# First attention: three quarters of the probabilities transposed by DMA in 16-bit halves

## The chip, the cores and the metric

The kernel runs on one core of a Trainium2 chip. The core has five engines, each with an instruction queue of its own that is worked in order: TensorE (matmuls and weight loads, PE and PEld in the profile), VectorE (DVE), ScalarE (ACT), GpSimd (POOL) and SyncE (SP, which issues most DMAs). An instruction waits on semaphores for what it needs; while it waits, everything behind it on the same engine waits too. The metric is the device time of one execution in microseconds.

## The reference

A trunk of two layers on 256 tokens of width 1024, all in float32: a layer of dilated attention, a layer of forgetting attention, each followed by a SwiGLU feed-forward part, and a last norm. The change touches the first attention alone:

```python
DILATED_PATTERNS = ((128, 1), (512, 4), (2048, 16))

def dilated_mixer(h, w_in, w_out):
    B, S, _ = h.shape
    proj = (h @ w_in).reshape(B, S, N_GROUPS, 3, N_HEADS, HEAD_DIM)
    ...
    for g, (window, dil) in enumerate(DILATED_PATTERNS):
        q = partial_rotary(proj[:, :, g, 0], pos)
        k = partial_rotary(proj[:, :, g, 1], pos)
        v = proj[:, :, g, 2]
        o, lse = dilated_band_attention(q, k, v, dil, window // dil)
        ...
    wts = jax.nn.softmax(jnp.stack(lses, axis=0), axis=0)
    o = jnp.einsum('gbsh,gbshd->bshd', wts, jnp.stack(outs, axis=0))
    return o.reshape(B, S, ATTN_WIDTH).astype(h.dtype) @ w_out
```

The softmax over the three groups' denominators makes the whole the same as one softmax over the scores of all three groups together, which is how the kernel computes it.

## The kernel before

**Units.** The 16 heads are worked in four quads of four heads, a quad in two pairs (`pr`) of two heads (`h`). The loop over `a_units` takes one piece of weights (1024 x 256 values) at a time: for each quad six q and k pieces (three groups, `rotated` behind each) and the value pieces. A piece comes by two DMAs of 512 KB into `raw` tiles (five of them), issued on SyncE. ScalarE makes its high part `wh` (L79) and VectorE its low part `wl` (L83), and TensorE multiplies three times (`mm3`: high by high, high by low, low by high). Four pieces fit into the `wh` and `wl` tiles, so a piece is split well ahead of its use.

**A projection** of q or k is 48 matmuls of 256 columns into one of two accumulators `ps_mm`. VectorE empties it with a shuffle (L441) and a multiply (L442), and only then can the projection after next start.

**Attention of a quad.** `scores_0` and `scores_12` put the scores of a head into one tile `p` of five blocks of 128 columns: block 0 and block 4 for the dilated groups, blocks 1 to 3 for the first group. `softmax_a` (ScalarE's L288 and L505, VectorE's L496 and L507) makes probabilities of them in place. `trans_a` transposes a pair's ten blocks on TensorE (L300) into PSUM and copies them out (L305: two copies of 512 columns on ScalarE, one of 256 on VectorE). `pv_a` multiplies them with the values (L312). Blocks of values for the dilated groups are put together by GpSimd, 16 copies a quad (L284, `values_12`).

**Order.** `later(i, ...)` puts a step behind unit `i`. Softmax stands behind the first unit after a quad's last q or k projection; the transposes of the two pairs stand behind two units some four units later, and PV behind the unit after these. A scheduler places each engine's instructions from that program order; work under `first()` goes ahead of other work that is ready. The instructions of an engine then run in that fixed order.

Of the kernel before, what the change touches and what calls it, by code (L numbers as in the profile page):

```python
# [9 lines left out]

F32 = mybir.dt.float32
F32R = mybir.dt.float32r
AF = mybir.ActivationFunctionType
ALU = mybir.AluOpType
AX = mybir.AxisListType

P = 128
D = 1024
S = 256
# [12 lines left out]
def trunk(ctx: ExitStack, tc: tile.TileContext, T, out):  # L32
    nc = tc.nc
# [3 lines left out]
    ap = ctx.enter_context(tc.tile_pool(name="ap", bufs=1))  # L37
# [258 lines left out]
    def transposed(blocks, copy=nc.vector.tensor_copy, tag="tr", home="pt"):  # L296

        tr = psum(tag)
        for i, b in enumerate(blocks):
            nc.tensor.transpose(tr[:, i * P:(i + 1) * P], b, ident)  # L300
        n = len(blocks) * P
        bufs, cols = {"pt": (3, 512), "bias": (4, 6 * P)}[home]
        w = ap.tile([P, cols], F32, tag=home, name="pt", bufs=bufs)
        with first():
            copied["last"] = copy(w[:, :n], tr[:, :n])  # L305
        return w

    def pv(o, v, kb, pr, w, n, start, stop):

        for h in range(2):  # L310
            c = kb * S + pr * P + h * HD
            nc.tensor.matmul(o[h * HD:(h + 1) * HD], v[:, c:c + HD], w(h), start=start, stop=stop)  # L312
# [6 lines left out]
    o = psum("o")  # L319
# [55 lines left out]
    for k in range(KT):  # L375
        if k % 4 == 0:
            w = tuple(wp.tile([P, 2048], F32R, tag=y, name=y, bufs=4) for y in ("wh", "wl"))
        g, u = g_a[:, k:k + 1], slice(k % 4 * 512, k % 4 * 512 + 512)
        with first(), in_order(cut):
            if k == 0:  # L380
                a = nc.vector.tensor_scalar(hi[:, k], xk[k], g, None, op0=ALU.mult)
            else:
                a = nc.scalar.activation(hi[:, k], xk[k], AF.Copy, scale=g)
# [4 lines left out]
        if k in (1, 5, 7):  # L388
            with first(), in_order(cut):
                a = [square(i) for i in {1: (0, 1), 5: (2,), 7: (3,)}[k]][-1]  # L390
# [12 lines left out]
    with first(), in_order(cut):  # L403
        a = square(4)
# [22 lines left out]
    x = []  # L427
# [81 lines left out]
    def trans_a(quad, pr):  # L509
# [5 lines left out]
                         transposed([block(h, 3) for h in range(2)], home=home),  # L515
                         transposed([block(h, b * 4) for h in range(2) for b in range(2)], nc.scalar.copy, "o", home)]

    def pv_a(quad, pr):
        vs, ws = quad["v"], quad["w", pr]
        o = psum("o")  # L520

        pv(o[:, :S], vs[0], 0, pr, lambda h: ws[0][:, h * S:(h + 1) * S], S, True, False)
        pv(o[:, P:S], vs[0], 1, pr, lambda h: ws[1][:, h * P:(h + 1) * P], P, False, False)
        halves = lambda x, a: x.rearrange("p (b n) -> p b n", b=2)[:, :, a * 32:a * 32 + 32]
        for a in range(4):
            pv(halves(o[:, :S], a), vs[1 + a % 2], a // 2, pr, lambda h: halves(ws[2][:, h * S:(h + 1) * S], a), 64,
               False, a == 3)
        src = o[:, :S].rearrange("p (b a u) -> p b a u", b=2, a=4)
        kt = quad["hq"] * 2 + pr
        split(ot, lambda x: x[:, kt, :].rearrange("p (b u a) -> p b a u", a=4, b=2), src)  # L530
# [3 lines left out]
    def later(i, fn, *a):  # L534
        due.setdefault(i, []).append((fn, a))

    quads = [{"hq": hq, "fm": {}, "pt": {}, "v": {}} for hq in range(4)]
    for i, (hq, g, w) in enumerate(a_units):
        quad = quads[hq]
        if i == 3:  # L540
            o = o_next
        elif i:

            wt = weights("a_in", hq * 9 + g * 3 + w, read if i > 4 else None)
        if i != 3 and (w < 2 or g == 0 and hq > 1):
            o = psum("mm")
        if i == 1:
            ident = const("ident", [P, P])
            rcos = const("rcos", [P, S])
            rsin = const("rsin", [P, S])  # L550
        if i == 2:
            mask0 = const("mask0", [P, 3 * P])
            mask12 = const("mask12", [P, S])
        if i in (24, 31):
            x.append(hrow("x"))
            t = len(x) - 1
            nc.sync.dma_start(x[t], T["x"][t * P:(t + 1) * P, :])
        if w < 2:
            for c in range(2):
                if i == 3 and c == 0:  # L560
                    continue
                proj_feat(xt, wt, o[:, c * S:(c + 1) * S], c, (KT // 2, rstd_a) if i == 2 and c == 1 else None)
            if i == 2:
                values_12(quad["v"], lead)

                second = []
                wt = weights("a_in", 1, second)
                second.pop(0)()
                o_next = psum("mm")
                rb = psum("tr")  # L570

                def rows():
                    for t in range(2):
                        nc.tensor.matmul(rb[:, t * P:(t + 1) * P], r_a[t].to_broadcast([P, P]), ident,
                                         start=True, stop=True)

                proj_feat(xt, wt, o_next[:, :S], 0, (6, rows))
                with first():
                    for c in (rcos, rsin):
                        nc.vector.tensor_tensor(c, c, rb[:, :S], op=ALU.mult)  # L580
            q, read = rotated(o, g, w)
            if i == 2:
                second.pop()(read)
            quad["fm"][g, w] = q
            if w == 1:

                j = i + (hq == 0)
                step = lambda hq: 9 * hq + 11 + 2 * (hq == 0)
                if g == 0:
                    later(step(hq - 1) + 2 if hq else j + 3, scores_0, quad)  # L590
                if g == 2:
                    later(j + 1, scores_12, quad)
                    later(j + 1, softmax_a, quad)
                    for pr in range(2):
                        later(step(hq) + pr, trans_a, quad, pr)
                    for pr in range(2):
                        later(step(hq) + 2, pv_a, quad, pr)
        elif g == 0 and hq > 1:
            for t in range(2):
                proj_tok(xt, wt, o[:, t * S:(t + 1) * S], t)  # L600
            quad["v"][0] = v_tile(o, r_a)
        elif i > 1:


            half = hq % 2 if g == 0 else g - 1
            if half == 0:

                lead = [psum("mm" if g else "o") for _ in range(2)]
            proj_pair(xt, wt, lead, half)
            if half and g == 0:  # L610
                vs = [v_tile() for _ in range(2)]
                for t in range(2):
                    v_pair(vs, lead[t], t, r_a[t])
                for y in range(2):
                    quads[hq - 1 + y]["v"][0] = vs[y]
            elif half:
                values_12(quad["v"], lead)
        for fn, a in due.pop(i, ()):
            fn(*a)
# [289 lines left out]
    ws = [weights("b_in", i * 3 + 2, ahead=2 - i) for i in range(2)]  # L909
    os = [psum("mm") for _ in range(2)]  # L910
    vs = [v_tile() for _ in range(3)]
# [27 lines left out]
    for i, (hq, w) in enumerate(b_units):  # L939
# [4 lines left out]
        o = psum("mm")  # L944
        if w < 2:
# [15 lines left out]
            if w == 1:  # L961
                j = i + 1
# [38 lines left out]
    parts, hg = [], []  # L1001
# [111 lines left out]
```

## Time and profile before

| | us |
|---|---|
| median of 3 runs | 742.76 (742.75 to 742.82) |
| the profiled execution | 742.78 |
| its span in the trace | 741.0 |
| VectorE busy | 489.5 |
| ScalarE busy | 375.5 |
| GpSimd busy | 65.0 |

The profile is of one execution. Its page lists each engine's busy time, the chain of work that ended last, groups of instructions (source line, engine, operation, output and inputs, count, busy time, mean) and the DMAs. The timeline gives single instructions: start, duration, engine, line, operation, count, and in brackets how long the engine had been idle and who ended that. In the list of waits a row says which instruction waited for which other, the total, how often, and the longest. TensorE's granted clock is at nine tenths of full speed or more in 39 of the span's 40 slices, and at eight in the last.

The DMA queues and what else the prediction needs are shown there.

### The profile page before, as it was taken

Reading aid. Unit: us, or ns where it says so; the run is one execution under the profiler, and the core shown is the slowest. Engines: PE = TensorE matmul, PEld = TensorE weight load, DVE = VectorE, ACT = ScalarE, POOL = GpSimd, SP = SyncE. Lnnn points to the kernel's source line nnn. Section 1 sums busy time; section 2 is a strip of 40 time slices with the busy share of each in tenths; the row PEclk is TensorE's granted clock in tenths of the full one; section 3 lists DMA queues with packets and bytes.
Section 4 is the critical chain, followed back from the end, with each engine's and each line's share of the span. In section 5 each row is a group of like instructions: output and inputs, shape, how many; then the busy total and the mean of one; then the engine's idle time right before and its main releaser. Section 6 shows DMA issues by size and latency. Waiting matters only on the chain.

```text
span 741.0 us, 14364 instructions
## 1 busy us (share of the span) xinstructions
PE 733.1 (99%) x5916; PEld 679.1 (92%) x5916; DVE 489.5 (66%) x768; ACT 375.5 (51%) x617; POOL 65.0 (9%) x106
## 2 busy tenths in 40 slices
PE   9999999999999999999999999999999999999996
PEld 7999989999988789999999988999889999999995
DVE  6997988787888575545556375586877455555533
ACT  7546437437436465445445354487565444445521
POOL 0600003005006010000000004110000000000001
PEclk9999999999999999999999999999999999999998
DMA  8865544644646267565567543785537655656601
GB/s 332 304 199 172 188 156 147 212 154 150 214 145 225 65 226 251 180 201 194 184 209 234 170 133 123 261 254 170 171 118 236 227 187 193 206 177 217 206 1 57
DMA packets 39297, 138.00 MB, mean 186 GB/s; under 512 B 4512, under 2 KB 5696, under 8 KB 39232
## 3 DMA queue, kind: packets, MB, share of 16 engines
q1 hardware_dynamic: 39088, 136.94, 56.0%
q8 instruction: 46, 0.75, 0.4%
q14 instruction: 19, 0.16, 0.1%
q10 hardware_dynamic: 144, 0.15, 0.1%
HBM read 136.00 MB, written 1.07 MB: 185 GB/s over the span
## 4 chain that ended last, share of the span: by engine, by line
PE 96%; ACT 1%; DMA 1%; DVE 1%; issue 0%; SPq 0%; POOL 0%; POOLq 0%; DVEq 0%; ACTq 0%
PE ps_mm L207 34%; PE ps_mm L202 17%; PE ps_tr L207 9%; PE ps_sc L207 8%; PE ps_o L207 7%; PE ps_tr L202 5%; PE ps_sc L202 4%; PE ps_o L202 4%; PE ps_o L312 2%; PE ps_tr L300 1%; DMA otl<-in_lead 1%; PE ps_sc L475 1%; PE ps_tr L195 1%; PE ps_o L300 1%; PE ps_sc L868 0%; PE ps_sc L457 0%
## 5 line engine op out<-in xcount | busy, mean ns | idle before, releaser
L79 ACT ACTIVATE wh<-raw 128x1024 fp32r<-128x1024 f32 x236 | 243.3, 1055 | 238.7 <-PE ps_tr L207 66.6
L83 DVE TENSOR_TENSOR wl<-raw,wh 128x1024 fp32r<-128x1024 f32 x236 | 285.1, 1228 | 82.7 <-ACT wh L79 82.4
L202 PE MATMUL ps_mm<-xt,wh 128*128 128x256 f32 x816 | 227.7, 279 | 0.0
L207 PE MATMUL ps_mm<-xt,wl 128*128 128x256 f32 x816 | 226.2, 277 | 0.1
L207 PE MATMUL ps_mm<-xt,wh 128*128 128x256 f32 x816 | 226.0, 277 | 0.0
L202 PEld LDWEIGHTS ps_mm<-xt,wh 128*128 128x128 f32 x816 | 153.4, 188 | 1.8 <-issue 1.7
L207 PEld LDWEIGHTS ps_mm<-xt,wl 128*128 128x128 f32 x816 | 153.5, 188 | 0.4 <-DVE wl L83 0.3
L207 PEld LDWEIGHTS ps_mm<-xt,wh 128*128 128x128 f32 x816 | 153.4, 188 | 0.0
L207 PE MATMUL ps_tr<-xt,wl 128*128 128x256 f32 x304 | 83.9, 276 | 0.0
L207 PE MATMUL ps_tr<-xt,wh 128*128 128x256 f32 x304 | 83.8, 276 | 0.0
L202 PE MATMUL ps_tr<-xt,wh 128*128 128x256 f32 x304 | 83.6, 276 | 0.0
L704 DVE TENSOR_TENSOR sa<-ps_tr,sa 128x256 f32<-128x256 f32 x38 | 16.1, 424 | 73.4 <-PE ps_tr L207 73.4
L207 PEld LDWEIGHTS ps_tr<-xt,wh 128*128 128x128 f32 x304 | 57.1, 188 | 0.0
L207 PEld LDWEIGHTS ps_tr<-xt,wl 128*128 128x128 f32 x304 | 57.1, 188 | 0.0
L202 PEld LDWEIGHTS ps_tr<-xt,wh 128*128 128x128 f32 x304 | 56.9, 188 | 0.0
L284 POOL COPY v<-v 32x256 f32<-32x256 f32 x64 | 38.0, 594 | 175.8 <-ACT v L280 173.1
L202 PE MATMUL ps_mm<-wh,xt 128*128 128x512 f32 (+1 forms) x144 | 49.7, 345 | 0.0
L207 PE MATMUL ps_mm<-wl,xt 128*128 128x512 f32 (+1 forms) x149 | 49.2, 336 | 0.0
L207 PE MATMUL ps_mm<-wh,xt 128*128 128x512 f32 (+1 forms) x149 | 49.2, 335 | 0.0
L172 POOL TENSOR_SCALAR rs<-ssq 128x1 f32<-128x1 f32 x7 | 3.1, 448 | 421.7 <-ACT junk L181 421.7
L202 PE MATMUL ps_sc<-wh,ah 128*128 128x512 f32 x80 | 31.4, 392 | 0.0
L207 PE MATMUL ps_sc<-wl,ah 128*128 128x512 f32 (+1 forms) x82 | 31.3, 385 | 0.0
(230 smaller groups left out, 1097.0 us busy)
## 6 DMA issues: line engine op xcount, KB each, us to landing
raw<-in_gu SPq DMA_DIRECT2D x88, 512.0 KB, 4.7
raw<-in_a_in SPq DMA_DIRECT2D x68, 512.0 KB, 4.4
raw<-in_dn SPq DMA_DIRECT2D x44, 512.0 KB, 4.7
raw<-in_b_in SPq DMA_DIRECT2D x24, 512.0 KB, 4.9
raw<-in_a_out SPq DMA_DIRECT2D x8, 512.0 KB, 5.2
raw<-in_b_out SPq DMA_DIRECT2D x8, 512.0 KB, 4.5
bias<-sums SPq DMA_DIRECT2D x8, 384.0 KB, 5.8
grow<-in_norms SPq DMA_DIRECT2D x4, 512.0 KB, 6.0
```

What stands on the lines that cost most here:

```text
L79: a = nc.scalar.activation(view(hi), src, AF.Copy)
L83: return nc.vector.tensor_tensor(view(lo), src, view(hi).bitcast(F32), op=ALU.subtract)
L172: nc.gpsimd.tensor_scalar(m, s, rest, None, op0=ALU.add)
L195: nc.tensor.transpose(tr[:, k * P:(k + 1) * P], xn[:, kk * P:(kk + 1) * P], ident)
L202: nc.tensor.matmul(o, sh, mh, start=start, stop=False)
L207: last = nc.tensor.matmul(o[:, u], s, m[:, u], start=False, stop=end and u.stop == n)
L284: nc.gpsimd.tensor_copy(v[1 + a % 2][n:n + 32, a // 2 * S:a // 2 * S + S], by_t[a * 32:a * 32 + 32, t, g])
L300: nc.tensor.transpose(tr[:, i * P:(i + 1) * P], b, ident)
L312: nc.tensor.matmul(o[h * HD:(h + 1) * HD], v[:, c:c + HD], w(h), start=start, stop=stop)
L475: nc.tensor.matmul(sc[h][c, o:o + 64], q[HR[h], pr, qb * P + a * 32:qb * P + a * 32 + 32], k[HR[h], pr].rearrange("p (b n) -> p b n", b=2) ...
L704: nc.vector.tensor_tensor(a, u, sg, op=ALU.mult)
```

## The change

For quads 0 to 2 the transposes leave TensorE. A new function `turn_a` stands directly behind the softmax (`later(j + 1, ...)`) in place of `trans_a`. For each of the four heads of a quad it does three things:

1. GpSimd copies the head's five blocks of float32 as 1280 16-bit halves, low halves of all elements first, then high halves (L528 in the changed kernel).
2. SyncE issues one transposing DMA of the ten 16-bit blocks of 128 x 128 into a tile `turned` (L530).
3. ScalarE copies the halves back into their places in 32-bit elements (L531), into the tile that held GpSimd's output.

`pv_a` reads its blocks from the new place. Quad 3 keeps `trans_a`. The tiles `pt` become 640 columns wide instead of 512, and `turned` uses the four tiles `bias`, one of which is free for the fourth head only when an earlier one has been read.

```diff
-        bufs, cols = {"pt": (3, 512), "bias": (4, 6 * P)}[home]
+        bufs, cols = {"pt": (3, 640), "bias": (4, 6 * P)}[home]
...
+    def turn_a(quad, pr):
+
+        quad["w", pr] = []
+        bufs = {"pt": 3, "bias": 4}
+        parts = lambda x: x[:, :640].bitcast(U16).rearrange("p (c t) -> p t c", t=2)
+        for h in range(2):
+            home = ("pt", "bias")[pr]
+            w = ap.tile([P, 640 if home == "pt" else 6 * P], F32, tag=home, name="pt", bufs=bufs[home])
+            split16 = w[:, :640].bitcast(U16)
+            nc.gpsimd.tensor_copy(split16.rearrange("p (t c) -> p t c", t=2), parts(quad["pt"][pr, h]))
+            turned = ap.tile([P, 6 * P], F32, tag="bias", name="turned", bufs=4)[:, :640].bitcast(U16)
+            nc.sync.dma_start_transpose(turned.rearrange("p (g c) -> p g c", c=P), split16)
+            nc.scalar.copy(parts(w), turned.rearrange("p (t c) -> p t c", t=2))
+            quad["w", pr].append(w)
...
+        if len(ws) == 2:
+            blocks = [w[:, :640].rearrange("p (i j) -> p i j", j=P) for w in ws]
+            straight = lambda h: ws[h][:, P:3 * P]
+            corner = lambda h: ws[h][:, 3 * P:4 * P]
+            dilated = lambda h, a: blocks[h][:, 0:5:4, a * 32:a * 32 + 32]
...
                     for pr in range(2):
-                        later(step(hq) + pr, trans_a, quad, pr)
+                        if hq == 3:
+                            later(step(hq) + pr, trans_a, quad, pr)
+                        else:
+                            later(j + 1, turn_a, quad, pr)
```

What this does to the engines' order is shown at three places. The first is SyncE's queue at quad 0's softmax, before (`raw` are halves of weight pieces):

```order
L100 DMA raw_980<-in_a_in 128x1024
L100 DMA raw_982<-in_a_in 128x1024
L100 DMA raw_1045<-in_a_in 128x1024
L100 DMA raw_1047<-in_a_in 128x1024
L100 DMA raw_1129<-in_a_in 128x1024
L100 DMA raw_1131<-in_a_in 128x1024
```

and the same weights in the changed kernel, with the four transposes (`turned`, one a head) between them:

```order
L101 DMA raw_1000<-in_a_in 128x1024
L101 DMA raw_1002<-in_a_in 128x1024
L101 DMA raw_1065<-in_a_in 128x1024
L530 DMA_TRANSPOSE turned_850<-pt_848 128x10x128
L530 DMA_TRANSPOSE turned_855<-pt_853 128x10x128
L530 DMA_TRANSPOSE turned_860<-pt_858 128x10x128
L101 DMA raw_1067<-in_a_in 128x1024
L101 DMA raw_1130<-in_a_in 128x1024
L530 DMA_TRANSPOSE turned_865<-pt_863 128x10x128
L101 DMA raw_1132<-in_a_in 128x1024
```

Three transposes now stand ahead of the second half of one piece, and the fourth ahead of the second half of the next. The second place is ScalarE's queue there, before (the last normalising of the softmax, then splits of weights and the copies out of PSUM):

```order
L505 ACTIVATE p_662<-p_662,c_826 128x384
L79 ACTIVATE wh_978<-raw_980 128x1024
L79 ACTIVATE wh_978<-raw_982 128x1024
L79 ACTIVATE wh_1043<-raw_1045 128x1024
L79 ACTIVATE wh_1043<-raw_1047 128x1024
L79 ACTIVATE wh_1127<-raw_1129 128x1024
L79 ACTIVATE wh_1127<-raw_1131 128x1024
L79 ACTIVATE wh_1211<-raw_1213 128x1024
L305 COPY pt_1113<-ps_tr_1108 128x512
```

and in the changed kernel:

```order
L506 ACTIVATE p_662<-p_662,c_826 128x384
L80 ACTIVATE wh_998<-raw_1000 128x1024
L80 ACTIVATE wh_998<-raw_1002 128x1024
L531 COPY pt_848<-turned_850 128x2x640
L531 COPY pt_853<-turned_855 128x2x640
L531 COPY pt_858<-turned_860 128x2x640
L80 ACTIVATE wh_1063<-raw_1065 128x1024
L80 ACTIVATE wh_1063<-raw_1067 128x1024
L80 ACTIVATE wh_1128<-raw_1130 128x1024
L531 COPY pt_863<-turned_865 128x2x640
```

The joining copies now stand ahead of the weights' splits that follow, three ahead of one piece and the fourth within the next; the copies out of PSUM are gone. The third place is GpSimd's queue from quad 1 into quad 2, in the changed kernel (`v` are blocks of values, `pt` the parted halves); before, only the value copies stood there:

```order
L528 COPY pt_1456<-p_1304 128x1280
L528 COPY pt_1461<-p_1306 128x1280
L528 COPY pt_2129<-p_1890 128x1280
L528 COPY pt_2134<-p_1892 128x1280
L285 COPY v_2221<-v12_2223 32x256
L528 COPY pt_2139<-p_1894 128x1280
L285 COPY v_2221<-v12_2223 32x256
L285 COPY v_2222<-v12_2223 32x256 x2
L285 COPY v_2221<-v12_2223 32x256 x2
```

Quad 2's third parting copy has a value copy ahead of it, and its fourth stands further down, behind 14 more.

More of the change, by code (lines that the diff above doesn't have):

```diff
@@ L12 @@
 F32R = mybir.dt.float32r
+U16 = mybir.dt.uint16
 AF = mybir.ActivationFunctionType
@@ L520, in pv_a @@
         o = psum("o")
-        pv(o[:, :S], vs[0], 0, pr, lambda h: ws[0][:, h * S:(h + 1) * S], S, True, False)
-        pv(o[:, P:S], vs[0], 1, pr, lambda h: ws[1][:, h * P:(h + 1) * P], P, False, False)
+        if len(ws) == 2:
[4 more added lines that the diff above has]
+        else:
+            straight = lambda h: ws[0][:, h * S:(h + 1) * S]
+            corner = lambda h: ws[1][:, h * P:(h + 1) * P]
+            dilated = lambda h, a: halves(ws[2][:, h * S:(h + 1) * S], a)
+        pv(o[:, :S], vs[0], 0, pr, straight, S, True, False)
+        pv(o[:, P:S], vs[0], 1, pr, corner, P, False, False)
         halves = lambda x, a: x.rearrange("p (b n) -> p b n", b=2)[:, :, a * 32:a * 32 + 32]
         for a in range(4):
-            pv(halves(o[:, :S], a), vs[1 + a % 2], a // 2, pr, lambda h: halves(ws[2][:, h * S:(h + 1) * S], a), 64,
-               False, a == 3)
+            pv(halves(o[:, :S], a), vs[1 + a % 2], a // 2, pr, lambda h: dilated(h, a), 64, False, a == 3)
         src = o[:, :S].rearrange("p (b a u) -> p b a u", b=2, a=4)
@@ L594, in trunk @@
                     for pr in range(2):
-                        later(step(hq) + pr, trans_a, quad, pr)
+                        if hq == 3:
+                            later(step(hq) + pr, trans_a, quad, pr)
+                        else:
+                            later(j + 1, turn_a, quad, pr)
                     for pr in range(2):
```

## The prediction

> **What bounds the kernel now.** I read the page's busy times first, then its chain of work, then the list of waits.
>
> ```profile
> PE 733.1 (99%) x5916; PEld 679.1 (92%) x5916; DVE 489.5 (66%) x768; ACT 375.5 (51%) x617; POOL 65.0 (9%) x106
> ...
> PE 96%; ACT 1%; DMA 1%; DVE 1%; issue 0%; SPq 0%; POOL 0%; POOLq 0%; DVEq 0%; ACTq 0%
> ...
> PE ps_o L321 <- DVE mhalf L65: 0.9, 1, 0.9
> ...
> 65.00:208.00 143.00, 143.00 (x1482) 136.25 (x1472) 118.51 (x200) 76.90 (x130) 15.75 (x32) 1.00 0.52 171
> ```
>
> TensorE is the bound: 99% busy, 96% of the chain, and one wait of 0.9 us in the whole program. The last row is the window of the first attention's three early quads: TensorE is busy through all 143 us (columns: PE, PEld, DVE, ACT, POOL, then clock 1.00 and DMA share 0.52), VectorE for 118.5, ScalarE for 76.9, GpSimd for 15.8. So work taken off TensorE here shortens the program at once, until another engine's result comes late.
>
> **What is removed.** Six pairs of heads (quads 0 to 2, two pairs each) lose ten transposes each, 60 in all. The timeline of TensorE shows one block of ten, the projection ahead of it, the one behind it, and the last two blocks:
>
> ```profile
> 81.49 0.28 PE L202 MATMUL ps_mm<-xt,wh 128*128 128x256 f32 x1
> ...
> 86.93 0.82 PE L300 MATMUL ps_tr<-ident,p 128*128 128x128 f32 x6
> 87.59 0.60 PE L300 MATMUL ps_o<-ident,p 128*128 128x128 f32 x4
> 87.94 0.36 PE L202 MATMUL ps_mm<-xt,wh 128*128 128x256 f32 x1
> ...
> 93.68 0.82 PE L300 MATMUL ps_tr<-ident,p 128*128 128x128 f32 x6
> ...
> 190.95 0.82 PE L300 MATMUL ps_tr<-ident,p 128*128 128x128 f32 x6
> ...
> 197.70 0.82 PE L300 MATMUL ps_tr<-ident,p 128*128 128x128 f32 x6
> ```
>
> A projection of 48 matmuls takes 86.93 − 81.49 = 5.44 us when no transposes stand ahead of it. From one block to the next it is 93.68 − 86.93 = 6.75 us, and again 197.70 − 190.95 = 6.75 us in quad 2. So a block costs 1.31 us: 87.94 − 86.93 = 1.01 us for the ten transposes, and 0.30 us because the projection behind them runs slower (93.68 − 87.94 = 5.74 us instead of 5.44). Six blocks: 6 x 1.31 = **7.9 us**; if the slower projections had another cause it would be 6 x 1.01 = 6.1 us. I take the whole, since the projection behind a block is slow in quad 2 as in quad 0, and the one ahead is not.
>
> Their evictions go too, from engines that are not the bound:
>
> ```profile
> L305 DVE COPY pt<-ps_tr x16: 411/551/692, 88.4 to 533.5; 128x256 f32<-128x256 f32 x8, 128x512 f32<-128x512 f32 x8
> L305 ACT COPY pt<-ps_tr 128x512 f32<-128x512 f32 x8 | 4.6, 574 | 3.8 <-PE ps_tr L300 3.8
> L79 ACT ACTIVATE wh<-raw 128x1024 fp32r<-128x1024 f32 x236 | 243.3, 1055 | 238.7 <-PE ps_tr L207 66.6 <-PE ps_mm L207 62.3 <-issue 50.0
> ```
>
> ScalarE loses 12 copies of 0.57 us, VectorE six of 0.41 us.
>
> **What is added, each twelve times.** *The joining copy on ScalarE*: 1280 elements. 512 take 0.574 us and 1024 take 1.055 us, 0.94 ns an element, so 1.055 + 256 x 0.94 ns = 1.30 us. The sum on ScalarE is 12 x (1.30 − 0.57) = 8.7 us in a window where it idles for 66. *The parting copy on GpSimd* (1280 16-bit elements) and *the transposing DMA* are in no row of this trace. The nearest:
>
> ```profile
> L284 POOL COPY v<-v x64: 390/397/1462, 25.7 to 237.4; 32x256 f32<-32x256 f32 x64
> 116.61 7.06 POOL L284 COPY v<-v 32x256 f32<-32x256 f32 x16 [79.18 <-ACT v L280]
> 173.86 10.03 POOL L284 COPY v<-v 32x256 f32<-32x256 f32 x16 [50.19 <-ACT v L280]
> ...
> q1 hardware_dynamic: 39088, 136.94, 56.0%
> ...
> raw<-in_a_in SPq DMA_DIRECT2D x68, 512.0 KB, 4.4
> ...
> bias<-sums SPq DMA_DIRECT2D x8, 384.0 KB, 5.8
> ...
> sums<-v SPq DMA_DIRECT2D x1, 16.0 KB, 1.5
> ```
>
> GpSimd's copy of 256 elements has a median of 0.397 us and a worst of 1.462 us. Five times as many elements give 2.0 us, and 7.3 us if every copy were like the worst; were two 16-bit elements worth one of 32 bits, 1.0 us. I take 2.0, from the median. The transposing DMA moves 128 x 1280 x 2 bytes, 0.33 MB. The weights' queue moved 136.94 MB in 56.0% of 741 us, 3.03 us a megabyte, so its packets would take 1.0 us of all engines if transposing cost nothing. From issue to landing, 512 KB take 4.4 us, 384 KB 5.8 and 16 KB 1.5. I take 4.4 us to landing with later ones overlapping; at the other end each waits for the one ahead, 5.8 us apiece. Twelve of them add 12 us of DMA time to a window whose share is 0.52. PV's matmuls keep their shapes and cost what they did.
>
> GpSimd's copies may slow VectorE meanwhile:
>
> ```profile
> 174.78 1.42 DVE L83 TENSOR_TENSOR wl<-raw,wh 128x1024 fp32r<-128x1024 f32 x1 [1.84 <-ACT wh L79]
> ```
>
> Beside value copies this `wl` took 1.42 us where others below take 1.22; some six such operations a quad are 1.2 us on VectorE, inside the margins worked out next.
>
> **What is queued behind them.** The three first joining copies of a quad stand in ScalarE's order ahead of the next weights' high parts (`wh`), those are waited for by VectorE's low parts (`wl`), and behind these stand the rotations that empty TensorE's accumulators. For quad 0:
>
> ```profile
> 71.25 1.91 ACT L505 ACTIVATE p<-p,c 128x256 f32<-128x256 f32 x4
> 73.07 2.00 ACT L79 ACTIVATE wh<-raw 128x1024 fp32r<-128x1024 f32 x2
> 76.14 1.06 ACT L79 ACTIVATE wh<-raw 128x1024 fp32r<-128x1024 f32 x1 [1.07 <-PE ps_mm L207]
> ...
> 72.71 1.26 DVE L507 TENSOR_SCALAR p<-p,c 128x256 f32<-128x256 f32 x4
> ...
> 83.53 1.22 DVE L83 TENSOR_TENSOR wl<-raw,wh 128x1024 fp32r<-128x1024 f32 x1
> ...
> 85.26 1.22 DVE L83 TENSOR_TENSOR wl<-raw,wh 128x1024 fp32r<-128x1024 f32 x1
> 87.14 0.74 DVE L441 STREAM_SHUFFLE rt<-ps_mm 128x512 f32<-128x512 f32 x1
> 87.78 0.67 DVE L442 TENSOR_TENSOR fm<-ps_mm,rcos 128x512 f32<-128x512 f32 x1
> ```
>
> *When it comes.* The first head's probabilities are ready at 72.2 (two of the four at 71.25). GpSimd's copies end at 74.2, 76.2 and 78.2; the third transpose lands at 78.2 + 4.4 = 82.6; its joining copy ends at 83.9. *When it is needed.* The `wh` of 76.14 and the one after it come behind that copy, and the `wl` of 83.53 and 85.26 behind those: VectorE uses them 7 us after ScalarE made them, and that lead is the cover. The shuffle and multiply of 87.14 to 88.45 free the accumulator that the projection after next needs at 93.68 − 1.31 = 92.37. Backwards: shuffle by 91.06, second `wl` by 89.84, two `wh` of 1.06 us before it, so the joining copies must end by 87.7. **Margin 3.8 us.** SyncE holds one piece of weights behind the third transpose; issued near 78.5 it lands near 83, before ScalarE comes to it.
>
> For quads 1 and 2:
>
> ```profile
> 171.32 1.91 ACT L505 ACTIVATE p<-p,c 128x256 f32<-128x256 f32 x4
> ...
> 184.36 1.21 DVE L83 TENSOR_TENSOR wl<-raw,wh 128x1024 fp32r<-128x1024 f32 x1
> 185.72 0.74 DVE L441 STREAM_SHUFFLE rt<-ps_mm 128x512 f32<-128x512 f32 x1
> ...
> 150.99 0.38 PE L202 MATMUL ps_mm<-xt,wh 128*128 128x256 f32 x1
> ```
>
> In quad 2 the third parting copy stands behind one value copy (10.03 / 16 = 0.6 us): it ends at 172.3 + 3 x 2.0 + 0.6 = 178.9, joined by 184.6. The shuffle of 185.72 may wait until 190.95 − 1.31 = 189.6, so the second `wl` must start by 188.4 and the joining end by 187.3: margin 2.7 us. In quad 1 GpSimd starts only behind the value copies at 116.61 + 7.06 = 123.7, joined by 135.4; the accumulator is needed at 150.99 − 2.62 = 148.4, so the limit is 143.8: margin 8.4 us. The fourth transpose of each quad comes later (in quad 2 behind 14 more value copies, near 190), but PV needs it only at about 202. So at my values all waits are hidden, and the sum is 742.78 (the profiled execution's own time; its span is 741.0, and the median shown is 742.76) − 7.9 = **734.9 us**.
>
> **The rivals.** *Transposes that don't overlap (the other side).* With 5.8 us each in turn, quad 0's third lands at 74.2 + 17.4 = 91.6, joined by 92.9, 5.2 us late; quad 2's at 174.3 + 17.4 + 1.3 = 193.0, 5.7 late; quad 1's at 144.4, 0.6 late. TensorE waits 11.5 us: 734.9 + 11.5 = **746.4**, slower. It decides from 3.9 us each (quad 2's limit), and from about 5.3 us the gain is gone, since each microsecond counts three times in two quads. For it: three are issued in a row on one queue. Against: 0.33 MB is 1.0 us at the queue's rate.
>
> *Blocks one after another.* A transpose has ten blocks of 128x128. If each were a small transfer of its own at the 1.5 us of the 16 KB row, a transpose takes 15 us: joined at 120.5, 172.0 and 220.6, late by 33, 28 and 33: **829 us**. Nothing in the trace speaks for it but the fixed part of small transfers. The Trainium skill, "VectorE: DVE Perf Modes", section "The three transpose paths", gives 1309 ns for one 128x128 block through the DMA crossbar against 390 on TensorE; no run here shows either, and were it paid ten times over, 13.1 us a transpose, the sum would be an estimated 812. Against it stands "Advanced Engine Details and Errata", section "X-Bar Transpose (TRN2)": such DMAs are as fast as plain ones, which no run here shows either and which would leave 734.9.
>
> *GpSimd is slow.* At 3.5 us a copy quad 2 is late by 1.8 us and quad 0 by 0.7: 737.4. At the worst row's 7.3 us, quads 0, 1 and 2 are late by 12, 8 and 13 us: 768. It decides from 2.9 us; the gain is gone from about 4.4. For it: the value copies' mean rises to 0.63 us beside VectorE's work.
>
> *The slower projections stay.* Then only the ten transposes go: 742.78 − 6.1 = 736.7.
>
> **How the numbers follow.** Forecast 0.42; slower projections stay 0.10; a few microseconds late, 737 to 741, 0.10; the lateness about equals the gain, 0.06; transposes that don't overlap 0.16; blocks one after another 0.09; GpSimd far slower 0.07. About 0.2% (1.5 us) is what a measurement can tell from no change. Faster: 0.42 + 0.10 + 0.10 = 0.62; within it 0.06; slower 0.32. The forecast's own range is 734 to 737. Both signs hold weight, so the range goes from 734.0 to 752, which takes in transposes of 5.8 us and a little beyond and leaves out the blocks, the slow GpSimd and the worst of the transposes that don't overlap.
>
> **What would show it.** Right: no wait of TensorE in the windows of the three quads; 5.44 us for every projection; transposes landing within 5 us and 2 us copies on GpSimd. Wrong: waits of TensorE on VectorE's rotations or `wl` at the second or third projection behind a quad's softmax, ScalarE idle until a transpose, and SyncE's weights issued late behind one.

## The result and the profile after

| | before | after |
|---|---|---|
| median, us | 742.79 (742.75 to 743.12, 4 runs) | 735.87 (735.11 to 736.28, 4 runs) |
| ratio | | 0.9905, interval 0.9888 to 0.9922 |
| span of the profiled execution, us | 741.0 | 734.3 |

The change makes the kernel 0.95% faster, 6.9 us, by the forecast mechanism and 1.0 us above the forecast 734.9. From the page of the changed kernel, the lines that answer to those of before:

```profile
PE 726.4 (99%) x5856; PEld 672.4 (92%) x5856; DVE 495.9 (68%) x762; ACT 388.7 (53%) x617; POOL 83.0 (11%) x118
...
DMA packets 55042, 141.93 MB, mean 193 GB/s; under 512 B 20257, under 2 KB 21441, under 8 KB 54977
...
q1 hardware_dynamic: 54832, 140.88, 59.4%
...
PE 97%; DVE 1%; ACT 1%; POOL 0%; issue 0%; POOLq 0%; DVEq 0%; ACTq 0%
```

Its list of waits for TensorE, whole, and the window of the three quads (columns as before: TensorE, its weight loads, VectorE, ScalarE, GpSimd, clock, DMA share):

```profile
PE ps_o L322 <- DVE mhalf L66: 0.9, 1, 0.9
PE ps_mm L203 <- ACT v L281: 0.2, 1, 0.2
...
65.00:208.00 143.00, 142.82 (x1463) 135.53 (x1464) 129.66 (x203) 90.33 (x131) 35.62 (x44) 1.00 0.67 201
```

TensorE is still the bound and still waits for almost nothing. Over the whole program VectorE's busy time rose from 489.5 to 495.9 us though six copies of 0.41 us left it and nothing came, so its other operations took about 9 us longer; that is read below. (In the window it is 11 us more, in part because work of the next stretch has moved up into it.) The three operations that the trace of before could not show, each by its line (nanoseconds minimum/median/maximum, then first and last start):

```profile
L528 POOL COPY pt<-p x12: 1247/1358/2245, 72.2 to 183.4; 128x1280 uint16<-128x1280 uint16 x12
...
L530 SPq DMA_TRANSPOSE turned<-pt x12: 1267/1366/1601, 73.8 to 185.0; - x12
...
DMA to landing us min/median/max: 3.3/3.5/5.8
...
L531 ACT COPY pt<-turned x12: 1647/1672/1698, 77.5 to 188.5; 128x1280 uint16<-128x1280 uint16 x12
```

And the timeline of quad 0, GpSimd, SyncE, ScalarE and VectorE, and the first matmul that needs the accumulator which VectorE's last row empties:

```profile
72.19 2.79 POOL L528 COPY pt<-p 128x1280 uint16<-128x1280 uint16 x2 [35.27 <-ACT p L506]
75.26 1.31 POOL L528 COPY pt<-p 128x1280 uint16<-128x1280 uint16 x1 [0.28 <-DVE p L508]
...
73.75 4.56 SPq L530 DMA_TRANSPOSE turned<-pt  x3
...
77.48 4.76 ACT L531 COPY pt<-turned 128x1280 uint16<-128x1280 uint16 x3 [2.60 <-DMA turned<-pt]
...
72.53 4.26 DVE L508 TENSOR_SCALAR p<-p,c 128x256 f32<-128x256 f32 x4
...
77.31 2.35 DVE L84 TENSOR_TENSOR wl<-raw,wh 128x1024 fp32r<-128x1024 f32 x2
...
80.23 0.66 DVE L443 TENSOR_TENSOR qk<-ps_mm,rcos 128x512 f32<-128x512 f32 x1
...
81.31 0.28 PE L203 MATMUL ps_mm<-xt,wh 128*128 128x256 f32 x1
```

The third joining copy ends at 82.24 us; the prediction had 83.9 and a limit of 87.7. But VectorE's normalising (L508) takes 4.26 us where the same four operations took 1.26.

**Where the time came from.** TensorE does the same 5856 matmuls in the same order in both kernels but for the transposes, so the starts of equal matmuls can be set side by side; the differences below are worked out from those starts (before less the other trace, us saved in a stretch of before's time). "Changed again" is the changed kernel profiled once more, beside a later set of runs.

| stretch of before | changed | changed again |
|---|---|---|
| start to 64.8 | 0.18 | −0.60 |
| quad 0, to 101.7 | 2.61 | 2.61 |
| quad 1, to 148.2 | 1.12 | 2.59 |
| to 171.4 | −0.01 | 0.00 |
| quad 2, to 205.7 | 2.62 | 2.62 |
| to the end | 0.14 | 0.14 |

A quad was to save 2 x 1.31 = 2.62 us, and does, in quads 0 and 2 and on the second look in quad 1. (On the second look the three quads give 7.8 us together, and 0.6 was lost ahead of them.) In the first profile quad 1 lost 1.5 of it. Two things are seen there. One is a gap in TensorE ahead of the first q projection:

```profile
114.14 0.40 PE L208 MATMUL ps_mm<-wh,xt 128*128 128x256 f32 x2
114.72 0.39 PE L203 MATMUL ps_mm<-xt,wh 128*128 128x256 f32 x1 [0.18 <-ACT v L281]
```

The other is the pace of the five projections behind it. First and last matmul of that run of 238 intervals, and then of quad 0's run of 286:

```profile
114.94 0.28 PE L208 MATMUL ps_mm<-xt,wh 128*128 128x256 f32 x1
...
142.97 0.28 PE L208 MATMUL ps_mm<-xt,wl 128*128 128x256 f32 x1
...
65.09 0.28 PE L208 MATMUL ps_mm<-xt,wh 128*128 128x256 f32 x1
...
97.52 0.28 PE L208 MATMUL ps_mm<-xt,wl 128*128 128x256 f32 x1
```

28.03 us / 238 = 117.8 ns from matmul to matmul, against 32.43 / 286 = 113.4 ns, with the granted clock at 1.00 in both. The 4.4 ns make 1.05 us over quad 1's run. Wherever the clock is at 1.00 in the traces of this case, a long run of such matmuls is at one of these two paces, from its first few intervals until something breaks it.

### The profile page after: what moved, and what is told of

It reads as the page before. It is cut to its first block, busy times and chain, and to the rows that moved or that the text cites. A ratio compares the mean times of both kernels' runs of the same rounds, so it can differ in the third digit from the quotient of the medians.

```text
span 734.3 us, 14310 instructions
## 1 busy us (share of the span) xinstructions
PE 726.4 (99%) x5856; PEld 672.4 (92%) x5856; DVE 495.9 (68%) x762; ACT 388.7 (53%) x617; POOL 83.0 (11%) x118
## 2 busy tenths in 40 slices
DMA packets 55042, 141.93 MB, mean 193 GB/s; under 512 B 20257, under 2 KB 21441, under 8 KB 54977
## 3 DMA queue, kind: packets, MB, share of 16 engines
HBM read 136.00 MB, written 1.07 MB: 187 GB/s over the span
## 4 chain that ended last, share of the span: by engine, by line
PE 97%; DVE 1%; ACT 1%; POOL 0%; issue 0%; POOLq 0%; DVEq 0%; ACTq 0%
PE ps_mm L208 34%; PE ps_mm L203 17%; PE ps_tr L208 9%; PE ps_sc L208 8%; PE ps_o L208 7%; PE ps_tr L203 5%; PE ps_sc L203 4%; PE ps_o L203 4%; PE ps_o L313 2%; PE ps_sc L395 2%; PE ps_tr L196 1%; PE ps_tr L301 1%; PE ps_sc L476 1%; PE ps_o L322 1%; PE ps_sc L894 0%; PE ps_sc L458 0%
## 5 line engine op out<-in xcount | busy, mean ns | idle before, releaser
L84 DVE TENSOR_TENSOR wl<-raw,wh 128x1024 fp32r<-128x1024 f32 x236 | 288.3, 1242 | 82.6 <-ACT wh L80 82.4
L208 PE MATMUL ps_tr<-xt,wh 128*128 128x256 f32 x304 | 83.9, 276 | 0.0
L208 PE MATMUL ps_tr<-xt,wl 128*128 128x256 f32 x304 | 83.9, 276 | 0.0
L285 POOL COPY v<-v 32x256 f32<-32x256 f32 x64 | 40.5, 632 | 71.2 <-ACT v L281 68.6
```

What stands on the lines that cost most here:

```text
L84: return nc.vector.tensor_tensor(view(lo), src, view(hi).bitcast(F32), op=ALU.subtract)
L208: last = nc.tensor.matmul(o[:, u], s, m[:, u], start=False, stop=end and u.stop == n)
L285: nc.gpsimd.tensor_copy(v[1 + a % 2][n:n + 32, a // 2 * S:a // 2 * S + S], by_t[a * 32:a * 32 + 32, t, g])
```

## The experiments

Four sets, each on one chip with runs of the kernel before beside it (medians there: 743.96 for the first four rows, 742.64 for the next four, 742.83 for three, 742.79 for the last). Ratios are to those.

| run | median, us | ratio to before, interval |
|---|---|---|
| no transposition | 737.75 | 0.9918, 0.9904 to 0.9931 |
| both ways at once | 744.16 | 1.0005, 0.9996 to 1.0014 |
| quads 0 and 2 only | 739.40 | 0.9939, 0.9926 to 0.9951 |
| values first in quad 1 | 735.95 | 0.9896, 0.9881 to 0.9911 |
| changed again | 735.52 | 0.9908, 0.9895 to 0.9922 |
| one transpose put back | 737.18 | 0.9926, 0.9913 to 0.9940 |
| parting copy four times | 775.26 | 1.0438, 1.0424 to 1.0452 |
| all quads by DMA | 741.28 | 0.9983, 0.9974 to 0.9992 |
| parting copy twice | 745.34 | 1.0034, 1.0023 to 1.0046 |
| seven pairs by DMA | 735.61 | 0.9907, 0.9894 to 0.9921 |
| seven pairs, values first | 734.81 | 0.9894, 0.9881 to 0.9908 |
| transposing DMA twice | 749.34 | 1.0081, 1.0065 to 1.0098 |

### No transposition at all

PV takes the probabilities as they lie: the whole of `turn_a` is left out, and the transposes too.

```diff
-            w = ap.tile([P, 640 if home == "pt" else 6 * P], F32, tag=home, name="pt", bufs=bufs[home])
...
-            nc.scalar.copy(parts(w), turned.rearrange("p (t c) -> p t c", t=2))
-            quad["w", pr].append(w)
+        quad["w", pr] = [quad["pt"][pr, h] for h in range(2)]
```

> Leaves out the transposition of quads 0 to 2 altogether (no GpSimd copy, no transposing DMA, no joining copy, no TensorE transpose; PV multiplies the probabilities as they lie). Theory: the added chain is hidden but for the 0.2 us wait of quad 1 and the five slower projections behind it (about 1.4 us in the changed kernel), so this run shows the bare gain on TensorE: 742.8 - 7.9 = 734.9, with every projection of the three quads at 113.3 ns a matmul. Rival 1: slower projections have another cause than transposes and waits: 736 to 737. Rival 2: the added chain costs TensorE several microseconds unseen: below 733.

737.75 us, nearest to the first rival: with less work it is no faster than the changed kernel. The two ratio intervals overlap, and the kernel before took 1.2 us more on this chip than in the first set, so it isn't shown to be slower either. By the starts of its matmuls it saves 1.36, 1.59 and 2.62 us in the three quads: the runs of quads 0 and 1 are at 117.8 ns here (286 and 243 intervals, 1.26 and 1.07 us) with neither a transpose nor any part of the new chain near them. So the slow pace does not need a transpose. Its span, 736.6, is 3.0 us above that of the changed kernel profiled again: 2.3 of these are the pace of the two runs, the rest lies outside the three quads.

### The transposes kept, the new chain beside them, unused

```diff
-                        if hq == 3:
-                            later(step(hq) + pr, trans_a, quad, pr)
-                        else:
+                        later(step(hq) + pr, trans_a, quad, pr)
+                        if hq < 3:
                             later(j + 1, turn_a, quad, pr)
```

Here the result of `turn_a` is thrown away.

> The transposes stay on TensorE as before, and the whole added chain (GpSimd copy, transposing DMA, joining copy) runs beside them for quads 0 to 2, its result unused. Theory: the chain alone costs TensorE at most one short wait, 742.8 to 743.6, with one wait of TensorE at most. Rival (the chain is paid for in contention): 745 or more.

Ratio 1.0005 (0.9996 to 1.0014): parting, transposing and joining, twelve times, cost nothing that can be measured. TensorE's only wait is the 0.9 us at the program's start. The normalising of quad 0, first without any chain (the run above), then with the unused one:

```profile
73.33 1.27 DVE L508 TENSOR_SCALAR p<-p,c 128x256 f32<-128x256 f32 x4
```

```profile
73.61 4.25 DVE L508 TENSOR_SCALAR p<-p,c 128x256 f32<-128x256 f32 x4
```

So it is the chain, and by its time GpSimd's copies, that stretches VectorE's work by 3.0 us; with GpSimd's copies doubled, and with the DMAs doubled, this is tried below. It was covered. Three of the six runs behind transposes were at 113.8 ns in this trace.

### Quads 0 and 2 by DMA, quad 1 on TensorE

```diff
-                        if hq == 3:
+                        if hq in (1, 3):
```

> Quad 1 keeps its transposes on TensorE; quads 0 and 2 use the DMA. Theory: quads 0 and 2 gain 2.6 us each, all of it: 742.8 - 5.2 = 737.6, quad 1's share of the change being only 1.5 to 2. Rival: each quad gives a third of the measured 6.9 us: 738.2. The rows that decide: pace of quad 1's projections (two slower ones behind its two transposes if the theory holds, five if quad 0's late weights are to blame whatever quad 1 does).

739.40 us, a gain of 4.6 on this chip's 743.96; both expectations were lower, reckoned from 742.8. By matmul starts quad 0 saves 1.36 (its run is at the slow pace), quad 1 0.00, quad 2 2.62. What a quad gives is its own.

### Quad 1's values ahead of its softmax

```diff
-                    later(j + 1, softmax_a, quad)
+                    late = 1 + (hq == 1)
+                    later(j + late, softmax_a, quad)
```

`turn_a` moves with it, and the first exponential is held behind the first copy of values (L281).

> The change, with one thing moved: in quad 1 ScalarE copies the first half of the values out of PSUM ahead of the first exponential, so that TensorE need not wait for the accumulator at the start of quad 1's next projection. Theory: no wait there, and the five projections of quad 1 run at 113.3 ns a matmul, not 117.8: 735.9 - 1.4 = 734.5. Rival (quad 1's projections are slow from traffic of GpSimd and the DMAs): only the wait goes, 735.5, and the pace stays 117.8.

The wait on L281 is gone and quad 1 saves its 2.62 us; but quad 0's run is slow this time (1.36), and the ratio cannot be told from the changed kernel's. The run behind it is at the fast pace here, as the theory said. But the gap does not decide the pace: quad 0's slow run has none ahead of it, and in the runs with four quads and with seven pairs by DMA, below, quad 1 has such a gap and a fast run. The gap was real, but its cost is within what a run's pace adds or takes.

### The changed kernel again, and with one transpose put back

```diff
+    def one_transpose(quad, pr):
+        tr = psum("tr")
+        nc.tensor.transpose(tr[:, :P], quad["pt"][pr, 0][:, :P], ident)
+        nc.vector.tensor_copy(ap.tile([P, 1], F32, tag="seen", name="seen", bufs=2), tr[:, :1])
...
+                        if hq < 3:
+                            later(step(hq) + pr, one_transpose, quad, pr)
```

> The changed kernel once more, beside the next three kernels on the same chip. Ratio to before 0.990 as in its first runs, 735.2 to 737.0 us. Theory (the pace of a run of projections, 113 or 118 ns between matmuls, is drawn anew at every break of the run, whatever makes the break): its three long runs of 238 to 286 intervals need not show the paces of the first profile (fast, slow, fast). Rival (the pace follows the program: the gap of 0.4 us in quad 1 makes it slow): fast, slow, fast again.

> The changed kernel with one transpose of 128x128 added on TensorE at each of the six old places, and a copy of one column of it on VectorE; its result isn't used. Prediction's term (the slower projection, 0.30 us, is made by a transpose standing ahead of it): six runs of 48 intervals turn slow, 6 x 0.30 us, and six transposes cost about 0.1 us each, so 2.4 us above the changed kernel beside it, near 738.3 us. Theory (the pace is drawn anew at a break): some of the six are slow and some fast, on the mean no dearer than the changed kernel's long runs, so 0.6 us above it for the transposes alone, 0 to 1.5.

The changed kernel repeats (0.9908), and its trace has all three long runs at 113.4 to 113.5 ns and no gap in quad 1: the first profile's slow quad was that execution's. With one transpose put back at each place, TensorE's timeline at the first two:

```profile
86.82 0.27 PE L536 MATMUL ps_tr<-ident,p 128*128 128x128 f32 x1
86.85 0.36 PE L203 MATMUL ps_mm<-xt,wh 128*128 128x256 f32 x1
...
92.59 0.27 PE L536 MATMUL ps_tr<-ident,p 128*128 128x128 f32 x1
92.61 0.36 PE L203 MATMUL ps_mm<-xt,wh 128*128 128x256 f32 x1
```

From block to block it is 92.59 − 86.82 = 5.77 us instead of 48 x 0.1134 = 5.44: 0.33 us for one transpose, of which 0.11 is the transpose and the matmul behind it and 0.2 the slow pace (47 x 4.4 ns). All six runs behind it are at 117.8 ns. Quads 0 and 2 each cost 0.65 us more, quad 1 1.21 (its run ahead of the first transpose was slow too); the medians differ by 1.66. This is between the two expectations, and nearer to the prediction's term. Counted over the profiles so far, 17 of 20 runs behind a transpose were slow, and of the 23 long runs of quads without one, over eight profiles (three that follow below included), 5. So a transpose makes the slow pace likely; what else sets it stays open.

### GpSimd's parting copy four times, and twice

```diff
             nc.gpsimd.tensor_copy(split16.rearrange("p (t c) -> p t c", t=2), parts(quad["pt"][pr, h]))
+            nc.gpsimd.tensor_copy(split16.rearrange("p (t c) -> p t c", t=2), parts(quad["pt"][pr, h]))
```

(three such lines for the first, one for the second).

> The changed kernel with GpSimd's parting copy made four times over, about 5.4 us a tile in place of 1.36. Theory (the prediction's limits: quad 0's third joining copy must end by 87.7 us, quad 2's by 187.3, and PV needs the fourth near 199): quad 0's third copy ends at 72.2 + 16.3 = 88.5, is joined 5.2 us later at 93.7, 6.0 late; quad 1's stays near its limit; quad 2's fourth stands behind 14 value copies and is joined near 205.7, 6 to 7 late. About 13 us above the changed kernel: 749, 745 to 751, with waits of TensorE on VectorE's rotations or low parts in quad 0 and on the joining copy in quad 2. Rival (the chain has so much room that GpSimd's time does not matter): 736.

> The changed kernel with GpSimd's parting copy made twice over. Made four times over it cost 39.7 us. Theory (the chain costs nothing until the joining copies end later than the limits worked out in the prediction, and then every late microsecond is paid): at 1.4 to 2.1 us a copy the third parting copy of quad 0 ends between 80.6 and 85.0 and is joined 5.2 us later, between 85.8 and 90.2, with the limit at 87.7; in quad 2 the third ends near 168.5 + 3 x 3.5 + 0.8 = 179.8, joined at 185.0 of 187.3, and the fourth, behind the value copies, near 196 of 199. So 0 to 3 us above the changed kernel: 735.5 to 738.5. Rival (each parting copy lies on the path, so that cost is in proportion, 39.7 / 3 for one more): 749.

775.26 and 745.34 us: 39.7 and 9.8 us above the changed kernel's 735.52, where about 13 and at most 3 were expected; the second run's rival, a cost in proportion (13), missed too. The smaller one shows why. VectorE and TensorE in quad 0 of the doubled copy:

```profile
72.63 5.24 DVE L508 TENSOR_SCALAR p<-p,c 128x256 f32<-128x256 f32 x4
77.79 1.73 DVE L445 TENSOR_TENSOR qk<-qk,rt 128x512 f32<-128x512 f32 x1
79.45 3.40 DVE L84 TENSOR_TENSOR wl<-raw,wh 128x1024 fp32r<-128x1024 f32 x2
...
83.40 0.67 DVE L443 TENSOR_TENSOR qk<-ps_mm,rcos 128x512 f32<-128x512 f32 x1
...
84.22 0.36 PE L203 MATMUL ps_mm<-xt,wh 128*128 128x256 f32 x1 [2.64 <-DVE qk L443]
```

TensorE waits 2.64 us for an accumulator that VectorE empties late, and nothing in VectorE's row of work from 72.63 to 84.07 depends on a joining copy: it is busy throughout, with 5.24, 1.73 and 3.40 us where the kernel before took 1.26, 0.68 and 2.35. Operations that read only PSUM, or PSUM and one tile (L443, here beside a GpSimd copy that lasts from 81.88 to 83.96), keep their 0.67 us. The Trainium skill, "SBUF — State Buffer", section "SBUF: two separate sides", says that GpSimd shares a pair of ports with those VectorE operations that run in a two-port mode or read two operands from SBUF, as a lock for a whole instruction; which of the operations here are slowed agrees with it.

The rest of the price comes behind the wait. Windows of the same trace (clock is the last column but two):

```profile
84.00:86.00 2.00, 1.78 (x11) 1.81 (x12) 2.00 (x3) 0.49 (x1) 1.76 (x1) 0.73 1.18 297
86.00:88.00 2.00, 2.00 (x11) 2.00 (x11) 2.00 (x3) 1.74 (x2) 0.00 (x0) 0.50 1.02 312
88.00:90.00 2.00, 2.00 (x18) 2.00 (x17) 2.00 (x5) 1.39 (x2) 0.00 (x0) 0.92 1.31 86
...
143.00:145.00 2.00, 1.63 (x14) 1.66 (x15) 2.00 (x4) 0.45 (x1) 0.00 (x0) 1.00 0.94 180
```

Behind a gap of 2.92 us in TensorE (from the start of one matmul to the start of the next) the granted clock is halved for 3.41 us: fifteen intervals between matmuls are 213 to 214 ns instead of 113, 1.5 us more. Behind a gap of 2.17 us, at 143 us, it stays at 1.00. Four gaps of 2.92, 2.17, 0.73 and 2.20 us and this one stretch make most of the 9.8. The Trainium skill, "TensorE: Matmul & The Clock Gate", section "Part 1: The HAM clock gate", says that the clock is halved after an idle window of about 3.4 us, comes back after a busy one, and that these windows run free of the program. The half clock lasts one such window here (84.93 to 88.34), but the gap that brought it on is shorter than one; on that the measurement decides. Length alone does not settle it either, as the run with all four quads shows below.

With four copies the waits are these:

```profile
PE ps_o L313 <- POOL v L285: 8.0, 4, 6.3
PE ps_o L313 <- ACT pt L534: 7.3, 2, 6.5
PE ps_mm L203 <- DVE fm L443: 6.7, 3, 3.2
PE ps_mm L203 <- DVE qk L443: 3.7, 1, 3.7
```

PV's waits on joining copies were among the limits worked out. Its 8.0 us on value copies, which GpSimd makes late, were not, and neither was the size of VectorE's slowing, with which the 10.4 us on its rotations came (how much of them is slowing and how much late weights isn't told apart). Around the gaps the granted clock was at 0.50 in four stretches, 27.3 us in all.

### Every transposing DMA twice

```diff
             nc.sync.dma_start_transpose(turned.rearrange("p (g c) -> p g c", c=P), split16)
+            nc.sync.dma_start_transpose(turned.rearrange("p (g c) -> p g c", c=P), split16)
```

> The changed kernel with every transposing DMA issued twice, into the same place; the joining copy waits for the second. GpSimd's copies stay single. In quad 0 the three second issues stand behind the first three on SyncE, 1.4 to 1.5 us each, so the third tile lands some 4.3 us later and is joined near 87, just inside the limit of 87.7; SyncE issues its weights 4 to 6 us later. That is as much delay for the third tile as the doubled parting copy made (9.8 us dearer in the two profiles). Theory now (what the doubled parting copy cost was VectorE's time: its operations run at half to a third of their pace beside GpSimd's copies, and the first rotation behind them comes late; delay alone has the room that the prediction worked out): 0 to 2 us above the changed kernel, 735.5 to 737.5, VectorE's normalising at 4.2 us as there. Rival (any delay of the chain costs): 744 to 746.

749.34 us, outside both expectations. Stretch by stretch it separates them. In quad 0 the third tile is joined 5.1 us later than in the changed kernel profiled again, while VectorE's normalising takes no longer than there:

```profile
79.25 4.53 SPq L531 DMA_TRANSPOSE turned<-pt  x3
...
86.44 1.67 ACT L532 COPY pt<-turned 128x1280 uint16<-128x1280 uint16 x1 [0.32 <-DMA turned<-pt]
...
73.36 4.25 DVE L508 TENSOR_SCALAR p<-p,c 128x256 f32<-128x256 f32 x4
```

The joining copy ends at 88.1, and quad 0 costs nothing (0.01 us by matmul starts), where the doubled parting copy cost 5.05. That is just inside the prediction's limit (87.7, or 88.35 here, where the quad starts 0.65 us later), and the third rotation then ends 0.5 us before TensorE needs its accumulator (92.50 of 93.02). Delay alone had the room that the prediction gave it; VectorE's slowing, not delay, was the price in the doubled parting copy's quad 0. And doubled DMAs leave the normalising at 4.25 us where doubled copies took it to 5.24, so it is GpSimd's copies that stretch it.

By matmul starts the 14.9 us of its span come later: 3.6 in quad 1, 8.0 between it and quad 2, none in quad 2, 3.2 behind it. The 8.0 begin here, at quad 1's PV:

```profile
152.69 2.39 PE L313 MATMUL ps_o<-pt,v 128*64 128x256 f32 x22 [4.76 <-ACT pt L532]
...
151.50:154.50 3.00, 1.81 (x19) 1.62 (x20) 2.24 (x4) 2.05 (x2) 0.00 (x0) 0.50 0.97 381
154.50:158.00 3.50, 3.50 (x26) 2.56 (x22) 0.31 (x1) 3.05 (x3) 0.00 (x0) 0.50 1.02 405
```

The second pair's PV waits for the fourth tile, and the granted clock (the last column but two) is 0.50 until 158.3, 6.8 us in all, which makes most of the rest of the 8.0. The fourth tile's parting copy has to wait until the first joining copy frees a tile (GpSimd waits 8.4 us for it), so what delays the first delays the fourth twice over, and SyncE's queue holds weights between its two issues. The prediction gave quad 1's margin for the third tile alone.

### The last quad by DMA, all of it and half of it

```diff
-                        if hq == 3:
+                        if hq == 3 and pr:
```

(for the half; for all of it, no pair keeps `trans_a`).

> The changed kernel with the fourth quad transposed by DMA too, so that no probabilities are transposed on TensorE in the first attention. Theory (what hides the chain is the room between softmax and PV, and the last quad has little): GpSimd is busy with value copies until 231.5 us, the second tile is joined near 239.5 and the fourth near 242, where PV would begin at 234; TensorE waits 5 to 8 us and saves 2.0 to 2.6, so 739 to 742 us. Rival (the chain is hidden in the last quad as well): 2.0 to 2.6 us below the changed kernel, near 733.6.

> The changed kernel with the first pair of the fourth quad by DMA too; its second pair stays on TensorE. With both by DMA the first pair's joining copies ended at 231.0 and 233.3 us and its PV began at 234.3, and the second pair's came late. Theory (what is joined before PV begins costs nothing): ten more transposes go, 1.0 us and up to 0.1 of slower matmuls behind them, against 0.4 us of a low part that came late in that run, so 0.3 to 1.1 us below the changed kernel, ratio to before 0.9895, near 734.9. Rival (the last quad has no room even for one pair): PV waits 1 to 3 us and it is 736 to 738.

> The kernel before this one, with quad 1's values brought to its place ahead of the softmax as well (the edit tried alone earlier, which took away a wait of 0.2 to 0.4 us of TensorE). Theory (both gains are real and small): 0.2 to 0.4 us below the one before it, ratio to before 0.989, near 734.5. Rival (a run's pace is drawn anew and hides so small a gain): no difference from it beyond its interval.

With all four quads it is 741.28 us, in the range expected. Joining copies, and PV, of the last quad, and the window behind:

```profile
229.38 1.66 ACT L531 COPY pt<-turned 128x1280 uint16<-128x1280 uint16 x1 [4.42 <-DMA turned<-pt]
231.62 1.65 ACT L531 COPY pt<-turned 128x1280 uint16<-128x1280 uint16 x1
236.15 1.61 ACT L531 COPY pt<-turned 128x1280 uint16<-128x1280 uint16 x1 [1.96 <-DMA turned<-pt]
238.58 1.60 ACT L531 COPY pt<-turned 128x1280 uint16<-128x1280 uint16 x1
...
234.28 1.33 PE L313 MATMUL ps_o<-pt,v 128*64 128x256 f32 x24
237.81 0.65 PE L313 MATMUL ps_o<-pt,v 128*64 128x256 f32 x2 [2.20 <-ACT pt L531]
240.23 2.40 PE L313 MATMUL ps_o<-pt,v 128*64 128x256 f32 x22 [1.77 <-ACT pt L531]
...
240.00:243.50 3.50, 3.27 (x24) 2.85 (x25) 0.80 (x2) 1.29 (x3) 0.00 (x0) 0.51 0.45 150
```

The first pair is joined 1.0 us before its PV, the second after it. TensorE waits 4.0 us for its joining copies, less than the 5 to 8 expected, and then has the granted clock at 0.50 for 3.4 us, though neither wait is longer than 2.20 us. In the traces' records of the granted clock every such stretch but the last, which runs into the program's end, lasts 3.41 us or two or three times that, and what lies between two of them is a whole number of such lengths. So whether a gap is paid twice depends on where it falls and on what other gaps lie near it, and not on its length alone; the exact condition is not shown here. With only the first pair moved (seven pairs) the time is 735.61, and 734.81 with quad 1's values first: the lowest median of the study. But their ratio intervals overlap the changed kernel's, so neither is shown to beat it, and the expected gain of 0.3 to 1.1 us isn't shown either.

## Why the prediction was right

**What bounds the kernel, and what is removed: right.** A quad saves 2.61, 2.59 and 2.62 us when its runs of projections are at the fast pace, against 2.62. The term of 0.30 us for a slower projection was rightly counted with the transposes: one transpose put back costs 0.33 us, most of it pace. What the prediction lacked is that the pace is no property of the place. A run no longer broken by transposes still starts at either pace, and, being five times as long, loses up to 1.26 us in one draw. In the first profile that and the gap of quad 1 took 1.5 us; in the run without any transposition the pace took 2.3. That is the 1.0 us between forecast and median, as far as the traces show; which pace the unprofiled executions had isn't known. The rival "the slower projections stay", 736.7, lies as far on the other side of the result.

**The added operations: hidden, as said, with sizes off both ways.** GpSimd's copy took 1.36 us, not 2.0; the DMA landed in 3.5 us, not 4.4, with three issued in 4.56 us and overlapping; the joining copy took 1.67, not 1.30: 1.3 ns for each 16-bit element, where a 32-bit one of the splits took 1.0. Why isn't shown. Together the third joining copy of quad 0 ended 1.7 us earlier than worked out. "Transposes that don't overlap" and "blocks one after another" fell with the landing times. By the 1309 ns a block that the prediction quoted from the Trainium skill, "VectorE: DVE Perf Modes", section "The three transpose paths", ten blocks would take an estimated 13.1 us; ten landed in 3.5. As for "as fast as plain ones", quoted there from the Trainium skill, "Advanced Engine Details and Errata", section "X-Bar Transpose (TRN2)": plain speed would be 1.0 us of all 16 DMA engines. The queue's share rose from 56.8% of 736.6 us (no transposition) to 59.2% of 733.6 (changed again), 15.9 us for twelve, 1.3 each; with every DMA issued twice it is 61.5% of 748.6, and the second twelve take 2.2 each. So by this share the transposing DMA is dearer than a plain one here, though too cheap to matter. Each adds (20257 − 4513) / 12 = 1312 packets of under 512 bytes (against the run without transposition).

**The step that failed: the margin.** "Margin 3.8 us" in quad 0 was worked backwards from the third rotation behind the softmax, the first whose low parts wait for the joining copies, and there it holds, as the doubled DMAs showed. The first of the three rotations stands right behind VectorE's normalising and was given no deadline. There the slowing by GpSimd had been put at 1.2 us a quad; the normalising alone lost 3.0. VectorE emptied that accumulator at 78.07 in the kernel before, and at 80.23 + 0.66 = 80.89 in the changed one, and TensorE's first matmul into it starts at 81.31. So the change went through with 0.4 us to spare, not 3.8, and one more copy on GpSimd was paid at once. The forecast held although the tightest place was not the one it guarded; that these 0.4 us were left was luck.

**The side effect seen and hardly paid.** ScalarE's waits for raw weights rose from 17.2 to 27.7 us (20.4 on the second look), since transposes stand ahead of weights on SyncE. In quad 1 the trace leads from there to TensorE's gap: ScalarE waits 1.6 us for a half of weights at 100.94, VectorE then 1.1 us for ScalarE's next result (`oth`), and from there to the softmax's maxima it works without a break; the first exponential waits for these, and the value copy stands behind it. Moving the values took the wait away, at no gain that could be measured.

## What to carry to other kernels

Work moved off the bound engine is worth what it took there, as long as every engine that it touches keeps its own deadline; so besides the new chain's own path, list the instructions that run beside it on an engine that it slows, and work each of their deadlines back too. A stream of equal matmuls may have more than one pace: look at the intervals before counting a slow stretch as the cost of what stands ahead of it, and look at two profiles. A wait of TensorE of 2 to 3 us can cost more than itself: look at the granted clock behind it.

## What the runs showed of the hardware

- Matmuls of 128 x 256 in fp32r that alternate with weight loads run 113.4 or 117.8 ns apart at a granted clock of 1.00, one or the other from the start of an unbroken run to its end, and the same run of the same kernel differs between two executions (quad 1: 117.8, then 113.4). What sets the pace is open.
- Four VectorE operations of 128 x 256 in place on SBUF take 4.26 us instead of 1.26 beside GpSimd copies of 1280 16-bit elements; those out of PSUM keep their time.
- After a gap of 2.9 us TensorE's granted clock was 0.50 for 3.4 us; after one of 2.2 us it stayed at 1.00, but two waits of 2.20 and 1.77 us close together halved it as well, and one of 4.76 us went with 6.8 us at 0.50.
- A transposing DMA of 128 x 1280 16-bit elements holds SyncE's queue for 1.37 us and lands in 3.5 us.
